# SwiGLU products and transposes later in their queues, activation sums between output-projection chunks, weight differences in place, in one layer on one Trainium2 core

## The chip, the core and the metric

The kernel runs on one core of a Trainium2 chip. The metric is the device time of one execution in microseconds (us); lower is better. Engines are named as in the profile: PE is TensorE's matmuls, PEld its weight loads, DVE is VectorE, ACT is ScalarE, POOL is GpSimd, and SP is SyncE, whose queue issues almost all loads.

## What is computed

The reference is one layer on 256 tokens of width 2048: a normalisation, an input projection into three token mixers (RWKV-7, gated delta rule, differential attention), an output projection with a residual, a second normalisation and a SwiGLU feed-forward part of hidden width 5632 with a residual. The change lies in the last third:

```
x = x + mixed @ w_out[l]
h = rms_norm(x, ffn_norm_w[l])
gate, up = jnp.split(h @ w_ffn_in[l], 2, axis=-1)
x = x + (jax.nn.silu(gate) * up) @ w_ffn_out[l]
```

All of it is in 32-bit floats.

## The kernel before, in words

**Products in three parts.** A 32-bit operand is split into a rounded part (hi, a cast on ACT) and a residual (lo, a subtraction on DVE), and a product is three matmuls: hi with hi, hi with lo, lo with hi. Each weight therefore goes through four steps: a load into a raw tile by SP's queue, the cast on ACT, the residual on DVE, and the matmuls of 128x128 by 128x512 on PE. The raw, hi and lo tiles rotate: 4 of each up to the feed-forward part, and there 5 raw (TILES["raw"] is 1), 8 hi and 8 lo.

**Before the feed-forward part.** The output projection has two halves of four chunks of 512 columns, oA and oB (the loop after `until("x2")`). After each chunk of oB, h2_cols (line 1220) is spawned: it turns the new columns of the residual stream by PE transposes and writes hTh and hTl, the split input of the feed-forward part. A spawned job is a Python generator; tick() moves every job one step, and a tick comes after each unit of weights, so a job's instructions stand between the units' instructions in the queues.

**The feed-forward part.** The hidden width is 11 chunks of 512. Chunk 0 is first_pair (line 1431): a gate projection and an up projection of 8 units each, 12 matmuls a unit. Chunks 1 to 10 are pair (line 1449, "pair 1" to "pair 10" below). A pair has 8 units of weights, each of two k-tiles of gate and up columns, and they alternate in kind. An S unit uses seven block products instead of eight, 21 matmuls; it needs sums of activation blocks and sums of weight blocks. An N unit has 24 matmuls and needs differences of activations. The seven partial results go to seven PSUM banks (four of mm, two of rw, one of gd) and are combined on DVE into the gate and up values of both token halves; ACT applies SiLU.

The groups in GROUPS say how the output products are interleaved: pair 1, four output units, pair 2, four output units, pair 3, eight output units, and so on with eight; after pair 10 come the last 24. An output unit (P) has two tiles of w_ffn_out and 12 matmuls.

**hid_cols** (line 1420) is spawned after each pair. Its first tick, after the next unit of PE work, multiplies gate by up (two DVE operations that write tile sg), the second and third tick turn the product by four PE transposes each into a gd bank, from which ACT and DVE write hidh and hidl, the split hidden values.

**Staging.** take_f (line 1339) is called ahead of each unit's matmuls and stages as many further units as the 8 hi and lo tiles allow; stage_one (line 1355) issues a unit's casts and residuals and load (line 1326) its successors' transfers. An N or P unit is a cast and a residual for each raw tile. An S unit (tiles b11, b12 | b21, b22) has four casts on ACT and seven operations on DVE: two that make b22 - b12 and that plus b11 in tile ta, two residuals, one that subtracts the sum from the second raw tile into tb, and the residuals of ta and tb.

**Activation sums.** ext_job (line 1395) is spawned before first_pair and makes the sums and differences of activations in 16 ticks, one pair of k-tiles in two ticks; finish(ej) runs what is left of it after first_pair.

**Order.** From `V.on = S.on = TE.on = True` on, that is in the whole feed-forward part, a helper (class Queue, line 98; its call is line 108, and nearly all instructions of the profile show that line) pins DVE, ACT and PE to the order in which the source issues instructions. The loop over seq sets that order:

```
            if ul is None:
                ej = spawn(ext_job())
                ab_ = first_pair(plan["first"])
                finish(ej)
            else:
                ab_ = pair(ul)
            spawn(hid_cols(ab_, hids[gi], j))
```

and in hid_cols the two multiplications come at the first step and a `yield` before each group of transposes. So in each queue a pair's multiplications stand after the first unit that follows the pair, and after what take_f staged ahead of that unit; the transposes stand after the second and the third.

Of the kernel before, what the change touches and what calls it, by code (L numbers as in the profile page):

```python
# [36 lines left out]
TILES = {"raw": 1, "hi": 4, "lo": 4}  # L37
# [116 lines left out]
def trunk(tc, A, out, dbg=None):  # L154
# [213 lines left out]
    lora = p_l.tile([P, 512], F32, name="lora")  # L368
    glora = p_l.tile([P, 512], F32, name="glora")
# [3 lines left out]
    gneps_c = C("eps")[:, 1:2]  # L373
    lnsc_c = C("eps")[:, 2:3]
# [93 lines left out]
    sgx = prq.tile([P, T], F32, name="sgx")  # L468
    bon = prq.tile([P, 4, T], F32, name="bon")
    Yt = prq.tile([P, 2, 512], F32, name="Yt")  # L470
    gns = prq.tile([P, 2, 24], F32, name="gns")
# [341 lines left out]
    cm_g2, pg2 = pool("gdn2", side="right")  # L813
    vtok = pg2.tile([P, 2, 4, 128], F32, name="vtok")
# [250 lines left out]
    def diff_evac(j, banks, res):  # L1065
        qns = []
        for t in range(2):
# [5 lines left out]
            ss = pd_.tile([P, 8], F32, tag="dss", name=nm("dss"), bufs=2)  # L1073
# [161 lines left out]

    until("x2")
# [3 lines left out]
    for key in ("oA", "oB"):  # L1240
        if key == "oB":
            finish(sj)
        for n in range(4):
# [16 lines left out]
    for cm in (cm_d, cm_mixrg, cm_rq, cm_tok, cm_l):  # L1260
        close(cm)
# [6 lines left out]
    NS = len(SEVEN)  # L1268
    sums_h = pf.tile([P, NS, 4, P], F32R, name="sums_h")
    sums_l = pf.tile([P, NS, 4, P], F32R, name="sums_l")  # L1270
    dif_h = pf.tile([P, KT // 2 - NS, 2, P], F32R, name="dif_h")
    dif_l = pf.tile([P, KT // 2 - NS, 2, P], F32R, name="dif_l")

# [35 lines left out]
    turn = {"raw": 0, "hi": 0, "lo": 0}  # L1309
    homes = {"raw": (p_raw, F32), "hi": (p_hi, F32R), "lo": (p_lo, F32R)}  # L1310

    def buf(kind):
        first, dt = homes[kind]
        i = turn[kind] % (4 + TILES[kind])
        turn[kind] += 1
        if i < 4:
            return first.tile([P, 1024], dt, tag=kind, name=nm(kind))
        return pf.tile([P, 1024], dt, tag=kind, name=nm(kind), bufs=TILES[kind])

    loaded, ready_w = {}, {}  # L1320
    at = {"load": 0, "stage": 0, "raw": 0, "cooked": 0, "used": 0}
# [4 lines left out]
    def load():  # L1326

        while at["load"] < len(queue) and at["raw"] + len(queue[at["load"]][1]) <= 4 + TILES["raw"]:
# [26 lines left out]
    def stage_one():  # L1355
# [3 lines left out]
        if kind != "S":  # L1359
            parts_ = [split(t) for t in r]  # L1360
            for x in parts_:
                x[2]()
            ready_w[u] = [half(x, j) for x in parts_ for j in range(2)]
        else:
# [15 lines left out]
            ready_w[u] = {"b11": half(s0, 0), "b21": half(s1, 0), "b22": half(s1, 1), "t3": half(sa, 0),  # L1380
                          "t2": half(sa, 1), "t4": half(sb, 0), "t1": half(sb, 1)}
# [3 lines left out]
        load()  # L1385

# [8 lines left out]
    def ext_job():  # L1395

        for q in range(KT // 2):
            x = pf.tile([P, 1024], F32, tag="ta", name=nm("xa"), bufs=1)[:, 0:2 * T].rearrange("p (k t) -> p k t", t=T)
            s_ = pf.tile([P, 512], F32, tag="u2", name=nm("xs"), bufs=1).rearrange("p (k t) -> p k t", t=P)
            V.tensor_tensor(x, hTh[:, 2 * q:2 * q + 2, :].bitcast(F32), hTl[:, 2 * q:2 * q + 2, :].bitcast(F32),  # L1400
                            op=ALU.add)
            if q in SEVEN:
                i = SEVEN.index(q)
                a11, a21, a12, a22 = x[:, 0, 0:P], x[:, 0, P:T], x[:, 1, 0:P], x[:, 1, P:T]
                V.tensor_tensor(s_[:, 0, :], a21, a22, op=ALU.add)
                V.tensor_tensor(s_[:, 2, :], a11, a21, op=ALU.subtract)
                V.tensor_tensor(s_[:, 1, :], s_[:, 0, :], a11, op=ALU.subtract)
                V.tensor_tensor(s_[:, 3, :], a12, s_[:, 1, :], op=ALU.subtract)
                h_, l_ = sums_h[:, i], sums_l[:, i]
            else:  # L1410
                i = [k for k in range(KT // 2) if k not in SEVEN].index(q)
                s_ = s_[:, 0:2, :]
                V.tensor_tensor(s_, x[:, :, 0:P], x[:, :, P:T], op=ALU.subtract)
                h_, l_ = dif_h[:, i], dif_l[:, i]
            yield
            S.copy(h_, s_)
            V.tensor_tensor(l_, s_, h_.bitcast(F32), op=ALU.subtract)
            yield
# [12 lines left out]
    def first_pair(ul):  # L1431
# [3 lines left out]
        for t in range(2):  # L1435
            sg = pf.tile([P, 512], F32, tag=f"sg{t}", name=nm("sg"), bufs=1)
# [3 lines left out]
        for i in range(len(uu)):  # L1440
            products(banks, uu, i, hx)
            if i == len(uu) - 4:
                load()
            if i == len(uu) - 2:
                stage_one()
            tick()
        return list(zip(sgs, banks))

    def pair(ul):
# [7 lines left out]
        for i, (u, q) in enumerate(ul):  # L1457
# [3 lines left out]
            if q in SEVEN:  # L1461
                e = SEVEN.index(q)
                s1, s2, s3, s4 = [(sums_h[:, e, j, :], sums_l[:, e, j, :]) for j in range(4)]
# [15 lines left out]
            if q == s_units[-1]:  # L1479
                c11 = pf.tile([P, 512], F32, tag="sg0", name=nm("sg"), bufs=1)  # L1480
                u2 = pf.tile([P, 512], F32, tag="u2", name=nm("u2"), bufs=1)
                u3 = pf.tile([P, 512], F32, tag="sg1", name=nm("sg"), bufs=1)
# [3 lines left out]
        c22 = pf.tile([P, 512], F32, tag="c22", name=nm("c22"), bufs=1)  # L1486
# [10 lines left out]
    for what, gi, j, ul in seq:  # L1497
        if what == "in":
            if j == 0:
                hids.append([pf.tile([P, 8, T], F32R, tag=tag, name=nm(tag), bufs=2) for tag in ("hidh", "hidl")])  # L1500
# [22 lines left out]
    for cm in (cm_f, R["x2"], cm_hT, cm_lo, cm_hi, cm_raw, cm_gdp, cm_rwp, cm_mm, cm_const):  # L1523
# [51 lines left out]
```

## Time and profile before

| | |
|---|---|
| median of 3 runs | 1238.4 us (1237.74 to 1238.54) |
| the profiled execution | 1237.4 us |
| its span, first to last instruction | 1235.5 us |
| PE busy | 1203.8 us, 97% |
| DVE busy | 946.6 us, 77% |
| ACT busy | 649.6 us, 53% |
| chain that ended last | PE 86%, DVE 8%, issue 3%, DMA 2%, ACT 2% |
| granted PE clock, mean | 0.995 |

The profile shows one execution. Busy time is the time in which an engine works on an instruction; matmuls are pipelined, and one that lasts 0.39 us can be followed by the next after less than that. An idle time of an engine carries the name of what ended it (the releaser). [...] The feed-forward part fills the span from about 493 us on; first_pair ends at about 537, pair 1 at 585, pair 2 at 643, pair 3 at 702.

### The profile page before, as it was taken

How to read it: one execution, taken by the hardware profiler on the slowest of the kernel's cores; microseconds unless marked ns; L12 is line 12 of the kernel's file. 1: busy time of each engine (PE TensorE's matmuls, PEld its weight loads, DVE VectorE, ACT ScalarE, POOL GpSimd, SP SyncE). 2: the span in 40 equal slices, each digit the busy share in tenths (PEclk: the TensorE clock that was granted, in tenths of full speed). 3: DMA queues.
4: the chain of work that ended last, by engine and by line, in shares of the span. 5: the costliest groups of instructions: out<-in, count | busy, mean ns of one | idle time of the engine just before them, and what ended most of it. 6: DMA issues, size and time to landing. Idle time of an engine off the chain costs nothing.

```text
span 1235.5 us, 16564 instructions
## 1 busy us (share of the span) xinstructions
PE 1203.8 (97%) x5942; PEld 985.9 (80%) x5942; DVE 946.6 (77%) x1310; ACT 649.6 (53%) x897; POOL 5.8 (0%) x11
## 2 busy tenths in 40 slices
PE   9999999999999999989898999999999999999998
PEld 7877888888888878868687788787878787878787
DVE  8585965699465767888989788887878796969852
ACT  7664454765456556645554445454645454545530
POOL 0100000000000000000000000000000000000000
PEclk9999999999999999999999999999999999999999
DMA  9755564256555536656465657475656565656761
GB/s 316 213 151 155 170 191 118 69 165 177 176 173 168 188 126 189 202 163 208 158 201 169 219 158 236 138 224 167 216 166 212 172 205 176 213 191 183 231 199 51
DMA packets 129201, 222.47 MB, mean 180 GB/s; under 512 B 19648, under 2 KB 24000, under 8 KB 129120
## 3 DMA queue, kind: packets, MB, share of 16 engines
q1 hardware_dynamic: 120960, 217.17, 56.4%
q10 hardware_dynamic: 8160, 4.27, 1.2%
q8 instruction: 46, 0.75, 0.2%
q14 instruction: 35, 0.29, 0.1%
HBM read 218.50 MB, written 2.88 MB: 179 GB/s over the span
## 4 chain that ended last, share of the span: by engine, by line
PE 86%; DVE 8%; issue 3%; DMA 2%; ACT 2%; DVEq 0%; SPq 0%; ACTq 0%
PE mm L108 71%; PE rw L108 9%; PE gd L108 6%; DVE lo L108 4%; DVE sg L108 2%; ACT hi L108 1%; DMA raw<-in_w_ffn_in 1%; DVE u L108 1%; DMA raw<-in_w_in 0%; DVE tb L108 0%; DMA vec<-in_vecs 0%; DVE c L108 0%; ACT s L108 0%; DVE ta L108 0%; DVEq L108 0%
## 5 line engine op out<-in xcount | busy, mean ns | idle before, releaser
L108 DVE TENSOR_TENSOR lo<-raw,hi 128x1024 fp32r<-128x1024 f32 (+2 forms) x410 | 461.6, 1152 | 134.0 <-ACT hi L108 133.5
L108 ACT CAST hi<-raw 128x1024 fp32r<-128x1024 f32 (+2 forms) x410 | 397.8, 994 | 259.3 <-PE mm L108 152.5
L108 PE MATMUL mm<-hi,hTh 128*128 128x512 f32 (+1 forms) x832 | 322.8, 394 | 1.0 <-ACT hi L108 1.0
L108 PE MATMUL mm<-lo,hTh 128*128 128x512 f32 (+1 forms) x832 | 317.1, 387 | 0.0
L108 PE MATMUL mm<-hi,hTl 128*128 128x512 f32 (+1 forms) x832 | 316.9, 387 | 0.0
L108 PEld LDWEIGHTS mm<-hi,hTh 128*128 128x128 f32 x832 | 155.4, 188 | 33.9 <-ACT hi L108 1.3
L108 PEld LDWEIGHTS mm<-hi,hTl 128*128 128x128 f32 x832 | 155.3, 188 | 32.4 <-issue 0.6
L108 PEld LDWEIGHTS mm<-lo,hTh 128*128 128x128 f32 x832 | 155.6, 188 | 30.9 <-issue 1.1
L108 PE MATMUL mm<-hi,hidh 128*128 128x512 f32 x352 | 140.8, 400 | 0.1
L108 PE MATMUL mm<-hi,hidl 128*128 128x512 f32 x352 | 138.6, 394 | 0.0
L108 PE MATMUL mm<-lo,hidh 128*128 128x512 f32 x352 | 138.6, 394 | 0.0
L108 PEld LDWEIGHTS mm<-hi,hidh 128*128 128x128 f32 x352 | 66.9, 190 | 16.5 <-issue 3.4
L108 PEld LDWEIGHTS mm<-hi,hidl 128*128 128x128 f32 x352 | 66.9, 190 | 14.5
L108 ACT CAST hi<-tb 128x1024 fp32r<-128x1024 f32 x40 | 42.2, 1054 | 68.8 <-DVE tb L108 67.2
L108 PEld LDWEIGHTS mm<-lo,hidh 128*128 128x128 f32 x352 | 66.8, 190 | 13.2
L108 ACT CAST hi<-ta 128x1024 fp32r<-128x1024 f32 x40 | 42.0, 1050 | 36.5 <-DVE ta L108 34.8
L108 DVE SCALAR_TENSOR_TENSOR xr<-mm,rst,xr 128x512 f32<-128x512 f32 x48 | 35.4, 748 | 27.5 <-PE mm L108 26.7
L108 DVE TENSOR_TENSOR lo<-tb,hi 128x1024 fp32r<-128x1024 f32 x40 | 49.0, 1225 | 3.7 <-ACT hi L108 1.3
L108 DVE TENSOR_TENSOR tb<-raw,ta 128x1024 f32<-128x1024 f32 x40 | 48.7, 1218 | 0.0
L108 DVE TENSOR_TENSOR lo<-ta,hi 128x1024 fp32r<-128x1024 f32 x40 | 48.7, 1217 | 0.0
L108 ACT CAST hidh<-gd 128x512 fp32r<-128x512 f32 x22 | 12.9, 587 | 62.1 <-PE gd L108 62.1
L108 DVE TENSOR_TENSOR hidl<-gd,hidh 128x512 fp32r<-128x512 f32 x22 | 15.2, 692 | 35.9 <-ACT hidh L108 35.8
(327 smaller groups left out, 1490.3 us busy)
## 6 DMA issues: line engine op xcount, KB each, us to landing
raw<-in_w_ffn_in SPq DMA_DIRECT2D x320, 256.0 KB, 3.2
raw<-in_w_in SPq DMA_DIRECT2D x103, 512.0 KB, 3.7
raw<-in_w_ffn_out SPq DMA_DIRECT2D x176, 256.0 KB, 3.9
raw<-in_w_out SPq DMA_DIRECT2D x32, 512.0 KB, 4.0
raw<-in_w_ffn_in SPq DMA_DIRECT2D x16, 512.0 KB, 3.9
raw<-in_w_in SPq DMA_DIRECT2D x9, 256.0 KB, 5.8
xr<-in_x SPq DMA_DIRECT2D x8, 256.0 KB, 5.4
out<-xr ACTq DMA_DIRECT2D x8, 256.0 KB, 2.1
```

The costliest lines, as they stand in the source:

```text
L108: r = call(*a, **kw)
```

## The change

- hid_cols gets an argument late. For pairs 1 to 10 it lets one tick pass ahead of the multiplications and one more ahead of the transposes: multiplications after the second following unit, transposes after the fourth and fifth. After first_pair the multiplications are issued at once (one step at spawn), the transposes stand where they stood.
- The activation sums move from ext_job into ext(n), which follows h2_cols(n) as one job (cols_ext) spawned after each chunk of oB, four k-tiles a part. The part of the last chunk runs in first_pair, which finishes it after the first unit of its up projection.
- In stage_steps (stage_one in steps) the weight differences of an S unit are written over the raw tiles; ta and tb are gone. The order of DVE is now difference, residual, sum, residual, subtraction, residual, residual. The first S unit is staged in steps during first_pair's up projection.
- Six raw tiles instead of five. To make room the pools of the earlier part stay open, and their tiles get new uses: sums and differences in old attention tiles, raw and lo tiles in the old constants and recurrence tiles, the hidden values alternately in an old and a new tile.
- The three epsilon columns get a DMA of their own into a small tile, behind that of the constants.

```diff
-TILES = {"raw": 1, "hi": 4, "lo": 4}
+TILES = {"raw": 2, "hi": 4, "lo": 4}
...
-    cst = p_l.tile([P, 1168], F32, name="cst")
-    eps_c = C("eps")[:, 0:1]
...
+    cst = p_l.tile([P, 1152], F32, name="cst")
+    eps_c, gneps_c, lnsc_c = drv[:, 48:49], drv[:, 49:50], drv[:, 50:51]
...
-        nc.sync.dma_start(cst[:, 0:CONST.shape[1] - P], A["const"][:, P:])
+        nc.sync.dma_start(cst, A["const"][:, P:P + 1152])
+        nc.sync.dma_start(drv[:, 48:51], A["const"][:, P + 1152:])
...
+    def ext(n):
+
+        x4 = prq.tile([P, 4, T], F32, tag="bon", name=nm("xa"))
+        s4 = prq.tile([P, 2, 4, P], F32, tag="Yt", name=nm("xs"))
+        V.tensor_tensor(x4, hTh[:, 4 * n:4 * n + 4, :].bitcast(F32), hTl[:, 4 * n:4 * n + 4, :].bitcast(F32),
+                        op=ALU.add)
+        yield
+        ss = []
+        for j, q in enumerate((2 * n, 2 * n + 1)):
+            x, s_ = x4[:, 2 * j:2 * j + 2, :], s4[:, j]
+            if q in SEVEN:
...
+            yield
+        for s_, h_, l_ in ss:
+            S.copy(h_, s_)
+            V.tensor_tensor(l_, s_, h_.bitcast(F32), op=ALU.subtract)
+            yield
+
+    def cols_ext(n):
+        yield from h2_cols(n)
+        yield
+        yield from ext(n)
...
             if key == "oB":
-                hj = spawn(h2_cols(n))
+                hj = spawn(cols_ext(n))
...
-            ta = pf.tile([P, 1024], F32, tag="ta", name=nm("ta"), bufs=1)
-            tb = pf.tile([P, 2, 512], F32, tag="tb", name=nm("tb"), bufs=1)
-            V.tensor_tensor(ta[:, 0:512], b22, b12, op=ALU.subtract)
-            V.tensor_tensor(ta[:, 512:1024], ta[:, 0:512], b11, op=ALU.add)
+            V.tensor_tensor(b12, b22, b12, op=ALU.subtract)
             s0[2]()
+            yield
+            V.tensor_tensor(b11, b12, b11, op=ALU.add)
             s1[2]()
-            sa = split(ta)
-            V.tensor_tensor(tb, r[1].rearrange("p (a c) -> p a c", c=512),
-                            ta[:, 512:1024].unsqueeze(1).to_broadcast([P, 2, 512]), op=ALU.subtract)
-            sb = split(tb.rearrange("p a c -> p (a c)"))
+            yield
+            sa = split(r[0])
+            two = r[1].rearrange("p (a c) -> p a c", c=512)
+            V.tensor_tensor(two, two, b11.unsqueeze(1).to_broadcast([P, 2, 512]), op=ALU.subtract)
+            yield
+            sb = split(r[1])
             sa[2]()
+            yield
             sb[2]()
...
-    def hid_cols(ab_, hid, c):
+    def hid_cols(ab_, hid, c, late):
+        if late:
+            yield
         for x, y in ab_:
             V.tensor_tensor(x, x, y, op=ALU.mult)
+        yield
         for i in range(2):
             yield
             b = gdbank(1)
...
             products(banks, uu, i, hx)
+            if i == 0:
+                finish(hj)
+                early = spawn(stage_steps())
             if i == len(uu) - 4:
+                at["limit"] = len(queue)
                 load()
             if i == len(uu) - 2:
+                finish(early)
                 stage_one()
             tick()
...
             if ul is None:
-                ej = spawn(ext_job())
                 ab_ = first_pair(plan["first"])
-                finish(ej)
             else:
                 ab_ = pair(ul)
-            spawn(hid_cols(ab_, hids[gi], j))
+            spawn(hid_cols(ab_, hids[gi], j, late=ul is not None), 0 if ul is not None else 1)
```

## Rows read from the trace of the kernel before

**Rows 1.** Page, part 1: busy us (share of the span) xinstructions.
```profile
PE 1203.8 (97%) x5942; PEld 985.9 (80%) x5942; DVE 946.6 (77%) x1310; ACT 649.6 (53%) x897; POOL 5.8 (0%) x11
```
**Rows 2.** Waits of PE: us in total, times, longest.
```profile
PE gd L108 <- DVE sg L108: 20.4, 20, 4.3
```
**Rows 3.** Timeline of PE, 540 to 710: start, us, what, [idle before, releaser].
```profile
545.19 0.76 PE L108 MATMUL mm<-hi,sums_h 128*128 128x512 f32 x1 [4.58 <-DVE sg L108]
...
595.23 0.30 PE L108 MATMUL gd<-ident,sg 128*128 128x128 f32 x1 [4.32 <-DVE sg L108]
...
653.14 0.30 PE L108 MATMUL gd<-ident,sg 128*128 128x128 f32 x1 [3.06 <-DVE sg L108]
...
709.63 0.30 PE L108 MATMUL gd<-ident,sg 128*128 128x128 f32 x1 [1.37 <-DVE sg L108]
```
**Rows 4.** Windows: length, busy PE, PEld, DVE, ACT, POOL, then clock, DMA share, GB/s.
```profile
545.00:550.00 5.00, 4.81 (x14) 3.86 (x15) 4.96 (x8) 1.09 (x2) 0.00 (x0) 0.66 0.82 262
595.00:600.00 5.00, 4.56 (x14) 3.58 (x15) 3.74 (x6) 2.48 (x3) 0.00 (x0) 0.66 0.00 1
653.00:658.00 5.00, 4.64 (x15) 3.63 (x16) 3.74 (x6) 2.48 (x3) 0.00 (x0) 0.66 0.00 0
709.00:714.00 5.00, 4.16 (x22) 3.41 (x23) 1.77 (x3) 0.67 (x2) 0.00 (x0) 1.00 0.60 201
464.00:496.00 32.00, 32.00 (x154) 26.38 (x153) 24.01 (x33) 21.76 (x40) 0.00 (x0) 1.00 0.63 185
...
1225.00:1230.00 5.00, 5.00 (x24) 4.14 (x23) 0.00 (x0) 0.00 (x0) 0.00 (x0) 1.00 0.00 0
```
**Rows 5.** Timeline of PE and DVE around the first two stalls.
```profile
539.53 0.69 DVE L108 TENSOR_TENSOR xa<-hTh,hTl 128x512 f32<-128x512 f32 x1
...
544.36 1.28 DVE L108 TENSOR_TENSOR sg<-sg,mm 128x512 f32<-128x512 f32 x2
...
585.21 0.47 PE L108 MATMUL mm<-hi,hidh 128*128 128x512 f32 x1
...
587.37 0.68 DVE L108 TENSOR_TENSOR ta<-raw,raw 128x512 f32<-128x512 f32 x1
...
595.00 0.68 DVE L108 TENSOR_TENSOR sg<-sg,c 128x512 f32<-128x512 f32 x1
```
**Rows 6.** The chain that ended last, in order of time: its last long piece.
```profile
1174.34 57.17 PE mm L108 x252
```
**Rows 7.** Tile xs: its DVE operations, ns min/median/max, first and last start, forms.
```profile
L108 DVE TENSOR_TENSOR xs<-xa x12: 282/292/426, 496.4 to 540.2; 128x128 f32<-128x128 f32 x8, 128x256 f32<-128x256 f32 x4
...
L108 DVE TENSOR_TENSOR sums_l<-xs,sums_h x4: 683/690/693, 500.7 to 531.1; 128x512 fp32r<-128x512 f32 x4
...
L108 DVE TENSOR_TENSOR dif_l<-xs,dif_h x4: 417/418/424, 506.4 to 541.1; 128x256 fp32r<-128x256 f32 x4
```
**Rows 8.** Tile raw: its loads.
```profile
DMA to landing us min/median/max: 2.6/3.8/8.3
```
**Rows 9.** Timeline of PE and DVE in pair 2, and around a transpose group.
```profile
603.68 0.39 PE L108 MATMUL rw<-hi,hTh 128*128 128x512 f32 x1
...
604.55 0.68 DVE L108 TENSOR_TENSOR ta<-raw,raw 128x512 f32<-128x512 f32 x1
...
610.03 1.22 DVE L108 TENSOR_TENSOR lo<-tb,hi 128x1024 fp32r<-128x1024 f32 x1
...
613.88 0.39 PE L108 MATMUL rw<-hi,hTh 128*128 128x512 f32 x1
...
658.38 0.60 PE L108 MATMUL gd<-ident,sg 128*128 128x128 f32 x4
...
659.64 0.69 DVE L108 TENSOR_TENSOR hidl<-gd,hidh 128x512 fp32r<-128x512 f32 x1 [0.50 <-ACT hidh L108]
```
**Rows 10.** DMA issues: KB each, median us to landing.
```profile
raw<-in_w_in SPq DMA_DIRECT2D x2, 4.0 KB, 3.2
```
**Rows 11.** Timeline of ACT: its first use of the constants.
```profile
37.20 0.26 ACT L108 ACTIVATE rst<-rw,cst 128x2 f32<-128x2 f32 x1 [4.14 <-PE rw L108]
```

More of the change, by code (lines that the diff above doesn't have):

```diff
@@ L467, in trunk @@
     cm_rq, prq = pool("rwq")
-    sgx = prq.tile([P, T], F32, name="sgx")
+    sgx = p_l.tile([P, T], F32, tag="xs1", name="sgx")
     bon = prq.tile([P, 4, T], F32, name="bon")
     Yt = prq.tile([P, 2, 512], F32, name="Yt")
-    gns = prq.tile([P, 2, 24], F32, name="gns")
     cm_rw, pr = pool("rwp")
@@ L813, in trunk @@
     cm_g2, pg2 = pool("gdn2", side="right")
+    gns = pg2.tile([P, 2, 16], F32, name="gns")
     vtok = pg2.tile([P, 2, 4, 128], F32, name="vtok")
@@ L1072, in diff_evac @@
             qn = p_tok.tile([P, 512], F32, tag="tok", name=nm("qn"), bufs=TOKB)
-            ss = pd_.tile([P, 8], F32, tag="dss", name=nm("dss"), bufs=2)
+            ss = (ssq, drv[:, 52:60])[t]
             act(qn, b, AF.Square)
@@ L1234, in h2_cols, with old, small @@
                                        op0=ALU.mult, op1=ALU.subtract)
+    def ext(n):
[8 more added lines that the diff above has]
+            if q in SEVEN:
+                a11, a21, a12, a22 = x[:, 0, 0:P], x[:, 0, P:T], x[:, 1, 0:P], x[:, 1, P:T]
+                V.tensor_tensor(s_[:, 0, :], a21, a22, op=ALU.add)
+                V.tensor_tensor(s_[:, 2, :], a11, a21, op=ALU.subtract)
+                V.tensor_tensor(s_[:, 1, :], s_[:, 0, :], a11, op=ALU.subtract)
+                V.tensor_tensor(s_[:, 3, :], a12, s_[:, 1, :], op=ALU.subtract)
+                ss.append((s_, *sums[SEVEN.index(q)]))
+            else:
+                i = [k for k in range(KT // 2) if k not in SEVEN].index(q)
+                s_ = s_[:, 0:2, :]
+                V.tensor_tensor(s_, x[:, :, 0:P], x[:, :, P:T], op=ALU.subtract)
+                ss.append((s_, dif_h[:, i], dif_l[:, i]))
+            yield
[7 more added lines that the diff above has]
+        yield from ext(n)
+    def old(tag, shape):
+        return pd_.tile(shape, F32R, tag=tag, name=nm("sums"), bufs=2)
+    def small():
+        return p_tok.tile([P, 512], F32, tag="tok", name=nm("sm"), bufs=TOKB)
     until("x2")
@@ L1242, in trunk @@
             finish(sj)
+            sums_h, sums_l = [[old(tag, [P, 2, 4, P]) for _ in range(2)] for tag in ("dqk0", "dqk1")]
+            dif_h, dif_l = [old("dv", [P, KT // 2 - len(SEVEN), 2, P]) for _ in range(2)]
+            sums = [(sums_h[i // 2][:, i % 2], sums_l[i // 2][:, i % 2]) for i in range(len(SEVEN))]
         for n in range(4):
@@ L1259, in trunk @@
     close(R["dr"])
-    for cm in (cm_d, cm_mixrg, cm_rq, cm_tok, cm_l):
-        close(cm)
     cm_f, pf = pool("ffn")
@@ L1307, in trunk @@
         seq.append(("out", gi, n, plan_out(n, 4 * (c0 - ng), 4 * ng)))
-    turn = {"raw": 0, "hi": 0, "lo": 0}
-    homes = {"raw": (p_raw, F32), "hi": (p_hi, F32R), "lo": (p_lo, F32R)}
+    first = {"raw": [(p_l, "loras", 1), (p_l, "cst", 1)], "hi": [], "lo": [(prq, "bon", 1), (prq, "Yt", 1)]}
+    homes = {}
+    for kind, old_ in (("raw", p_raw), ("hi", p_hi), ("lo", p_lo)):
+        more = TILES[kind] - len(first[kind])
+        homes[kind] = first[kind] + [(pf, kind, more)] * more + [(old_, kind, 4)] * 4
+    turn = {kind: 0 for kind in homes}
     def buf(kind):
-        first, dt = homes[kind]
-        i = turn[kind] % (4 + TILES[kind])
+        home, tag, n = homes[kind][turn[kind] % len(homes[kind])]
         turn[kind] += 1
-        if i < 4:
-            return first.tile([P, 1024], dt, tag=kind, name=nm(kind))
-        return pf.tile([P, 1024], dt, tag=kind, name=nm(kind), bufs=TILES[kind])
+        return home.tile([P, 1024], F32 if kind == "raw" else F32R, tag=tag, name=nm(kind), bufs=n)
     loaded, ready_w = {}, {}
-    at = {"load": 0, "stage": 0, "raw": 0, "cooked": 0, "used": 0}
+    at = {"load": 0, "stage": 0, "raw": 0, "cooked": 0, "used": 0, "limit": 1}
     def need(u):
@@ L1326, in load @@
     def load():
-        while at["load"] < len(queue) and at["raw"] + len(queue[at["load"]][1]) <= 4 + TILES["raw"]:
+        while at["load"] < min(len(queue), at["limit"]) and at["raw"] + len(queue[at["load"]][1]) <= 4 + TILES["raw"]:
             tiles = []
@@ L1385, in stage_one @@
         load()
+    def stage_one():
+        for _ in stage_steps():
+            pass
     def triple(bank, a, w, start, stop):
@@ L1435, in first_pair @@
         for t in range(2):
-            sg = pf.tile([P, 512], F32, tag=f"sg{t}", name=nm("sg"), bufs=1)
+            sg = small()
             act(sg, bg[t], AF.Silu, scale=rs2[:, t:t + 1])
@@ L1462, in pair @@
                 e = SEVEN.index(q)
-                s1, s2, s3, s4 = [(sums_h[:, e, j, :], sums_l[:, e, j, :]) for j in range(4)]
+                s1, s2, s3, s4 = [(sums[e][0][:, j, :], sums[e][1][:, j, :]) for j in range(4)]
                 f7, l7 = q == s_units[0], q == s_units[-1]
@@ L1479, in pair @@
             if q == s_units[-1]:
-                c11 = pf.tile([P, 512], F32, tag="sg0", name=nm("sg"), bufs=1)
-                u2 = pf.tile([P, 512], F32, tag="u2", name=nm("u2"), bufs=1)
-                u3 = pf.tile([P, 512], F32, tag="sg1", name=nm("sg"), bufs=1)
+                c11 = small()
+                u2 = small()
+                u3 = small()
                 S.copy(c11, p1)
@@ L1485, in pair @@
                 V.tensor_tensor(u3, u2, p7, op=ALU.add)
-        c22 = pf.tile([P, 512], F32, tag="c22", name=nm("c22"), bufs=1)
+        c22 = small()
         V.tensor_tensor(c11, c11, p2, op=ALU.add)
@@ L1499, in trunk @@
             if j == 0:
-                hids.append([pf.tile([P, 8, T], F32R, tag=tag, name=nm(tag), bufs=2) for tag in ("hidh", "hidl")])
+                hids.append([(p_mixrg, pf)[gi % 2].tile([P, 8, T], F32R, tag=tag, name=nm(tag), bufs=1)
+                             for tag in ("mixh_a", "mixl_a")])
             if ul is None:
-                ej = spawn(ext_job())
                 ab_ = first_pair(plan["first"])
-                finish(ej)
             else:
                 ab_ = pair(ul)
-            spawn(hid_cols(ab_, hids[gi], j))
+            spawn(hid_cols(ab_, hids[gi], j, late=ul is not None), 0 if ul is not None else 1)
         else:
@@ L1522, in trunk @@
                     nc.scalar.dma_start(out_v[t][:, 512 * j:512 * (j + 1)], o)
-    for cm in (cm_f, R["x2"], cm_hT, cm_lo, cm_hi, cm_raw, cm_gdp, cm_rwp, cm_mm, cm_const):
+    for cm in (cm_f, R["x2"], cm_d, cm_mixrg, cm_rq, cm_tok, cm_l, cm_hT, cm_lo, cm_hi, cm_raw, cm_gdp, cm_rwp, cm_mm, cm_const):
         close(cm)
```

39 lines of the change are left out of this document (5 added, 34 removed).

## The prediction

> **What bounds the kernel now.** I read the engine line of the page first: TensorE (PE) is busy 1203.8 us of the 1235.5 us span, 97% [rows 1]. So at most 32 us can come from removing waits, whatever VectorE (DVE) or the DMA queues save, unless matmuls themselves run faster. The second view is the list of PE's waits: 20 waits of gd on DVE sg add up to 20.4 us [rows 2]. The gd matmuls behind sg are the transposes of hid_cols, and sg is what its SwiGLU multiplications write. The third view, PE's timeline, says where: one stall of 4.58 us behind the first pair, in which mm waits for sg, then for gd one behind pair 1 (4.32), one behind pair 2 (3.06), and one of about 1.37 behind each of pairs 3 to 10, of which one stands here; each transpose group has a second wait of about 0.21 for the second multiplication, counted in the 20.4 [rows 3]. The fourth view is the granted clock. [...]
>
> Why sg is late is seen in DVE's queue, whose order the source fixes in this stage. Pair 1's output units start on PE at 585.21, and the transposes stand behind the second of them. DVE first ends pair 1's additions, then runs all seven operations of the next S unit from 587.37, and only then the two multiplications, which end at 595.68 [rows 5]. A unit of 12 matmuls is 12 x 226.9 ns = 2.72 us by the last stretch of the chain, 252 matmuls in 57.17 us [rows 6]; two units are over at 590.7, and PE waits.
>
> [...] I take PE as the bound.
>
> **The change, part by part.** Transposes later. With late set, a pair's multiplications are issued after the second following unit instead of the first, and its transposes after the fourth and fifth instead of the second and third. That adds 2 x 2.72 = 5.4 us of PE work ahead of the transposes and moves the multiplications behind at most one more staged unit. Pairs 3 to 10 have no S unit between, so their 1.37 us vanish with 4 us to spare. For pairs 1 and 2 four units end at 585.21 + 10.9 = 596.1; the multiplications ended at 595.7 [rows 5] and may end some 0.4 later, since in place the second subtraction stands behind a residual that waits for ScalarE's cast. Between nothing and 0.7 us each is left; I take 0.3, together 0.6. Removed: 20.4.
>
> First pair. The multiplications are now issued at its end, ahead of pair 1's first unit. Before, the last of the activation sums, started again at 539.53, and two residuals stood ahead of them until 544.36 [rows 5], while the sixth product group waited for the bank that they read. That bank is wanted after 15 matmuls (3.4 us); two multiplications take 1.28 us [rows 5]. Removed: 4.6.
>
> Clock. Without the three stalls longer than 3 us, nothing there lowers it: 3 x 5 us x (1 - 0.66) = 5.1 us [rows 4]. The 1.37 us stalls give none back.
>
> Activation sums earlier. A part for four k-tiles is one 128x1024 addition of some 1.22 us, as such operations take [rows 9], four 128x128 operations of 0.29, one 128x256 of 0.42, and residuals of 0.69 and 0.42 [rows 7], 3.9 us on DVE. Of the four parts, two and the addition of a third fall between output-projection chunks: 2 x 3.9 + 1.2 = 9.0 us. DVE was busy 24.0 of 32 us there [rows 4], so it is asked for 33.0: one us too much. Weights are staged three units ahead, 8.2 us, of which cast and residual take some 2.3, so a backlog of up to 5.9 us is covered. Cost taken: 0. Uncovered it would be from 1.0 to 9.0 us, plus 1.7 for the clock; a gain is excluded, since PE never waits there now. The rest falls in the first pair, where DVE loses 9.0 us of work; staging the first S unit early needs only tiles that are long free.
>
> Weight differences in place. The same seven DVE and four ACT operations; nothing is saved. The two raw tiles of an S unit are held to its end instead of partly freed after the first residuals, and the sixth raw tile answers that: three two-tile units instead of two are in hand, and SyncE's queue asks for a unit while two others, over 9 us of DVE work, are still to be staged, against a landing of 3.8 us [rows 8]. Cost taken 0; bounds 0 and 3.8 us for each of 40 S units.
>
> Pairs 2 and 3's second S unit. After the two short output groups the second transpose now stands behind the first unit of the next pair, and DVE and ACT can't stage the next S unit before it. That staging began at 604.55, 0.9 us after PE's unit at 603.68; now it begins after that unit (4.8 us), four transposes, a cast and a residual: a transpose group at 658.38 has its residual started at 659.64 and done 0.7 later [rows 9]. So it is some 6 us later. Its last residual ended at 611.25, and PE wants that group 3.4 us after 613.88 [rows 9], also 0.4 later now. 617.7 - 617.3 = 0.4 us to spare. Cost taken 0; bounds 0 and 2 us for each of two pairs.
>
> Epsilon columns. They get a small DMA of their own on SyncE's queue behind the constants. No row shows one of 12 bytes a partition; the nearest is one of 4 KB in all, 3.2 us to landing [rows 10]. ACT's first use waited 4.14 us for PE, not for the constants [rows 11], which covers that; behind it stand the identity and the low-rank weights, which are used later. Cost taken 0; bounds 0 and 3.2 us. GpSimd's queue is passed by nothing. The other moves of tiles issue nothing.
>
> **Sum.** 20.4 + 4.6 + 5.1 - 0.6 = 29.5 us. The profiled execution took 1237.4 us (1.9 beside its span), 1.0 under the median of 1238.4. Against the profile that is 1207.9, against the median **1208.9 us**.
>
> **Rivals.** *VectorE too full between output-projection chunks*: the 1.0 us overrun grows past the staging lead and PE waits there. For it: 33.0 of 32. Against: DVE's idle time before may also have been spent on work that can slide. 1208.9 + 2.7 to 10.7, some 1215.
>
> *A new wait at pairs 2 and 3* for the late S unit: 0.4 us to spare is less than my reckoning is good for. Up to 2 x 2 us, and 1.7 of clock for each stall if it becomes long: 1210 to 1216.
>
> *Slower: raw tiles come back too late.* An S unit (604.55 to 611.25) and an N unit's two residuals take DVE 6.7 + 2 x 1.22 = 9.1 us, and PE 10.2 (603.68 to 613.88 [rows 9]). If the longer hold lays a landing of 3.8 us [rows 8] open in each couple, it takes 12.9; 40 couples by 2.7 cost 108 us, and the time is 1317. It decides from 29.5 / 40 = 0.74 us a couple. Against it: the sixth tile, and a lead of over 9 us.
>
> *Nothing moves*: the hardware order stays, or another resource paces PE. The time is 1238. Against: the order in this stage is the source's, and [rows 4, 6].
>
> **How the numbers follow.** Forecast 0.70, full VectorE 0.13, pairs 2 and 3 0.08, slower 0.05, nothing 0.04. A difference under 0.2%, some 2.5 us, can't be told from none. The first three cases are faster: 0.91; same 0.04; slower 0.05. Low end: all waits gone without the 0.6, and 1.8 us for what the runs scatter and for the 2 us that PE still idles at the start: 1206.5. High end: 1217, which takes in the second rival and most of the first; the two last, 0.09, and the first's tail stay out.
>
> **What would show it.** Right: no gd on sg in PE's waits, the clock at 1.00 from 540 to 660, the multiplications straight behind the first pair, the sums' rows from about 475 to 515, and a distance of 64.2 instead of 65.8 us between the stalls' former places. Full VectorE: waits of PE on hi or lo before 500. Raw tiles: ACT or DVE waiting for DMA raw. The prediction is wrong if PE's idle time in sum stays over 12 us, or if matmuls start more than 227 ns apart without a wait.

## The result and the profile after

The changed kernel takes 1211.66 us (median of 4 runs, 1208.73 to 1212.23) against 1238.45 us: a ratio of 0.978 [0.9763, 0.9797] (the brackets hold a 95% interval, here and below), 26.8 us less. The forecast was 1208.9, with 1206.5 to 1217.0. The direction and the range hold; the point is 2.8 us too low. The profiled execution took 1212.02 us.

Two lines of the page of after: the engine line, which answers to [rows 1], and the chain.

```profile
PE 1198.6 (99%) x5942; PEld 985.1 (81%) x5942; DVE 942.7 (78%) x1306; ACT 650.2 (54%) x897; POOL 5.8 (0%) x11
...
PE 87%; DVE 6%; DMA 3%; issue 2%; ACT 2%; SPq 0%; DVEq 0%; ACTq 0%
```

PE is still the bound, now at 99%. The waits of PE in after (us in total, times, longest) answer to [rows 2]:

```profile
PE mm L108 <- DVE sm L108: 3.3, 2, 3.0
PE mm L108 <- ACT hi L108: 1.5, 1, 1.5
PE rw L108 <- DVE xs L108: 1.2, 1, 1.2
PE mm L108 <- DVE xr L108: 1.0, 1, 1.0
PE rw L108 <- DVE s L108: 0.3, 1, 0.3
```

All 20 waits of gd on the multiplications are gone. (Tiles share old homes now: sm stands for sg, mixh_a and mixl_a for hidh and hidl, sums for sums_h, sums_l, dif_h and dif_l.) Two waits are new and not small, and PE's timeline has them at two hand-offs, the start of pair 2 and the end of pair 3; it answers to [rows 3] (its first row, the transposes behind pair 1, has no wait):

```profile
590.97 0.60 PE L108 MATMUL gd<-ident,sm 128*128 128x128 f32 x4
...
595.96 0.47 PE L108 MATMUL mm<-hi,sums 128*128 128x512 f32 x1 [0.96 <-DVE xr L108]
...
690.12 0.77 PE L108 MATMUL mm<-hi,mixh_a 128*128 128x512 f32 x1 [2.98 <-DVE sm L108]
690.68 0.63 PE L108 MATMUL mm<-lo,mixh_a 128*128 128x512 f32 x1
691.11 0.63 PE L108 MATMUL mm<-hi,mixl_a 128*128 128x512 f32 x1
```

Behind the second of them matmuls start 0.43 us apart, against 0.227 [rows 6]. Windows of after, with the columns of [rows 4]:

```profile
464.00:496.00 32.00, 32.00 (x154) 26.38 (x153) 29.60 (x49) 23.05 (x42) 0.00 (x0) 1.00 0.64 193
...
690.00:692.00 2.00, 1.88 (x5) 1.52 (x6) 2.00 (x4) 0.72 (x1) 0.00 (x0) 0.50 1.05 390
692.00:694.00 2.00, 2.00 (x6) 1.61 (x5) 0.37 (x1) 1.60 (x3) 0.00 (x0) 0.50 0.71 261
694.00:696.00 2.00, 2.00 (x6) 1.52 (x6) 1.91 (x2) 1.00 (x2) 0.00 (x0) 0.50 0.04 16
696.00:698.00 2.00, 2.00 (x10) 1.62 (x9) 1.66 (x3) 0.00 (x0) 0.00 (x0) 0.96 0.76 243
```

The three low-clock stretches of [rows 4], with a mean of 0.66, are gone (1.00 from 540 to 550, 595 to 600 and 653 to 658), but after the new 2.98 us stall PE runs some 6 us at a granted clock of 0.50, half of full speed (690.12 to about 696.1). That costs about 2.9 us: the eight output units behind pair 3 take 25.69 us, where those behind pairs 4 to 9 take 22.84. The first window is the stretch of oB: DVE is busy 29.6 of 32 us there (24.0 before), and PE waits for nothing.

**Where the time went.** The table takes each block from its first matmul in PE's timeline to the first matmul of the next. O1 is the output units behind pair 1, and so on; "forecast" puts the terms of the prediction where they belong.

| block | before, us | after, us | gain | forecast |
|---|---|---|---|---|
| up to first_pair | 492.57 | 493.27 | -0.70 | 0 |
| first_pair and pair 1 | 92.64 | 86.71 | 5.93 | 6.3 |
| O1 and pair 2 | 18.47 + 40.80 | 11.35 + 42.61 | 5.31 | 5.93 |
| O2 and pair 3 | 17.09 + 40.97 | 11.24 + 44.94 | 1.88 | 4.67 |
| O3 | 24.81 | 25.69 | -0.88 | 1.58 |
| pair 4 to the last output chunks, 7 waits | 504.15 | 490.33 | 13.82 | 11.06 |
| sum | | | 25.4 | 29.5 |

The sum is that of the two profiled executions; before's lies 1.05 us under its median and after's 0.36 over, which makes the 26.8. Two rows carry the miss (O2 with pair 3, and O3: 5.3 us), and one gives 2.8 back.

**What a wait is worth.** O4 to O9 shrink from 24.81 to 22.84, 1.97 us for each pair of waits, which I had put at 1.37 + 0.21 = 1.58. PE's timeline of before, around the stall whose row stands in [rows 3], shows why:

```profile
707.87 0.39 PE L108 MATMUL mm<-hi,hidl 128*128 128x512 f32 x1
...
710.14 0.55 PE L108 MATMUL gd<-ident,sg 128*128 128x128 f32 x3 [0.21 <-DVE sg L108]
710.44 0.48 PE L108 MATMUL mm<-hi,hidh 128*128 128x512 f32 x1
...
713.28 0.60 PE L108 MATMUL gd<-ident,sg 128*128 128x128 f32 x4
713.64 0.48 PE L108 MATMUL mm<-hi,hidh 128*128 128x512 f32 x1
```

The unhindered group of transposes takes 713.64 - 713.28 = 0.36 us, and a matmul ahead of it 0.23, so the way from the last matmul to the next output matmul is 0.59 us. Behind the wait it took 710.44 - 707.87 = 2.57: 1.98 us lost, 0.40 more than the idle time. An idle time counts from the modelled end of a matmul (0.39 us behind its start), 0.16 after the point where the next would have started in the rows ahead (0.23 behind it). The other 0.24 went at the restart of the transposes: from the first of them at 709.63 to the output matmul at 710.44 are 0.81 us, less the second wait of 0.21 that is 0.60, against the unhindered 0.36.

### The profile page after: what moved, and what is told of

Same layout as the page of the kernel before. It is cut to its first block, busy times and chain, and to the rows that moved or that the text cites. A ratio compares the mean times of both kernels' runs of the same rounds, so it can differ in the third digit from the quotient of the medians.

```text
span 1210.0 us, 16543 instructions
## 1 busy us (share of the span) xinstructions
PE 1198.6 (99%) x5942; PEld 985.1 (81%) x5942; DVE 942.7 (78%) x1306; ACT 650.2 (54%) x897; POOL 5.8 (0%) x11
## 4 chain that ended last, share of the span: by engine, by line
PE 87%; DVE 6%; DMA 3%; issue 2%; ACT 2%; SPq 0%; DVEq 0%; ACTq 0%
PE mm L108 74%; PE rw L108 9%; PE gd L108 5%; DVE lo L108 3%; DMA raw<-in_w_ffn_out 1%; DVE raw L108 1%; ACT hi L108 1%; DMA raw<-in_w_ffn_in 1%; DMA raw<-in_w_in 1%; DVE xr L108 0%; DVE sm L108 0%; DMA vec<-in_vecs 0%; ACT s L108 0%; ACT mixh_a L108 0%; DVE mixl_a L108 0%
## 5 line engine op out<-in xcount | busy, mean ns | idle before, releaser
L108 ACT CAST hi<-raw 128x1024 fp32r<-128x1024 f32 (+1 forms) x490 | 478.5, 1004 | 336.3 <-DVE raw L108 127.9
L108 DVE TENSOR_TENSOR lo<-raw,hi 128x1024 fp32r<-128x1024 f32 (+1 forms) x490 | 558.8, 1164 | 115.1 <-ACT hi L108 109.6
L108 PE MATMUL mm<-hi,mixh_a 128*128 128x512 f32 x416 | 166.4, 400 | 3.3 <-DVE sm L108 3.3
L108 PE MATMUL mm<-hi,mixl_a 128*128 128x512 f32 x416 | 163.3, 393 | 0.0
L108 PE MATMUL mm<-lo,mixh_a 128*128 128x512 f32 x416 | 163.1, 392 | 0.0
L108 PE MATMUL mm<-hi,sums 128*128 128x512 f32 x320 | 118.2, 390 | 1.1 <-DVE xr L108 1.0
L108 PEld LDWEIGHTS mm<-hi,mixh_a 128*128 128x128 f32 x416 | 78.8, 189 | 23.4 <-issue 7.9
L108 PEld LDWEIGHTS mm<-hi,mixl_a 128*128 128x128 f32 x416 | 78.8, 189 | 17.0
L108 PEld LDWEIGHTS mm<-lo,mixh_a 128*128 128x128 f32 x416 | 78.9, 190 | 15.6
L108 DVE TENSOR_TENSOR raw<-raw,raw 128x512 f32<-128x512 f32 x80 | 76.3, 954 | 1.3
```

What stands on the lines that cost most here:

```text
L108: r = call(*a, **kw)
```

## The experiments

Every time is a median, beside a median of the kernel before on the same chip (1238.6, 1239.7 or 1239.2 us). The hand-off theory of the expectations: the late transposes themselves make the hand-offs to pairs 2 and 3 late, since their residuals stand ahead of staging in DVE's queue. Its rivals are the raw-hold theory (the longer hold of the raw tiles) and chance.

**after_again**: the changed kernel, unchanged.

> The changed kernel once more. Two theories of what kept it 2.8 us above the forecast, where the profile shows PE waiting 0.96 us for xr in pair 2 and 2.98 us for sm at the end of pair 3, with 3 us at the low clock behind the latter. Hand-off theory: the residual of the second transposes stands behind the first unit of pairs 2 and 3, VectorE stages all of the pair late, raw tiles come back late and the output weights land late; every execution has both waits, 1211 to 1212. Raw-hold theory: holding raw tiles to the end of an S unit makes the loads of output weights late in itself; every execution has the wait at the end of pair 3, 1211 to 1212. Rival of both, chance: the landing of a few transfers varies, and an execution without the long wait and its low clock takes 1206 to 1209.

1209.7 us (1208.61 to 1212.2), 0.9766 [0.975, 0.9781]. The two new waits recur. PE's timeline of this run:

```profile
594.68 0.47 PE L108 MATMUL mm<-hi,sums 128*128 128x512 f32 x1 [0.96 <-DVE xr L108]
...
689.90 0.77 PE L108 MATMUL mm<-hi,mixh_a 128*128 128x512 f32 x1 [4.04 <-DVE sm L108]
```

and its windows behind the second:

```profile
690.00:692.00 2.00, 2.00 (x5) 1.62 (x6) 2.00 (x4) 0.51 (x1) 0.00 (x0) 0.50 0.96 327
692.00:694.00 2.00, 2.00 (x8) 1.56 (x8) 0.27 (x2) 1.83 (x3) 0.00 (x0) 0.76 0.30 111
694.00:696.00 2.00, 2.00 (x11) 1.65 (x10) 2.00 (x2) 0.79 (x1) 0.00 (x0) 1.00 0.01 2
```

The waits belong to the kernel, not to one execution: every profile below that keeps the late transposes behind pair 2 and the staging ahead has a stall at the end of pair 3. The low clock behind the longer stall is shorter here, about 3 us. The eight executions of both labels sort by the clock: three at a mean clock of 1.000 took 1208.6 to 1209.0 us, three at 0.996 or 0.997 took 1212.0 to 1212.2, two at 0.999 lie between. A high clock doesn't mean that the long wait is absent: raw_five below has it (2.71 us) in an execution at 1.000.

**late_alone**: before, with the late steps of hid_cols alone; sums, weight differences and raw tiles as they were.

```diff
-            spawn(hid_cols(ab_, hids[gi], j))
+            spawn(hid_cols(ab_, hids[gi], j, late=ul is not None))
...
+        if late:
+            yield
         for x, y in ab_:
             V.tensor_tensor(x, x, y, op=ALU.mult)
+        if late:
+            yield
```

> The kernel before with one part of the change: for pairs 1 to 10 the multiplications one unit and the transposes two units later. Prediction's terms: the waits of gd on sg go (20.4 us) and two of the three stretches at the low clock (3.4), while the 4.6 us stall behind the first pair and its 1.7 us stay: 1238.5 - 23.8 = 1214.7. Theory that each wait also cost a restart of 0.4 us (the eight short ones took 1.97 us of block length for 1.58 of wait): 4 us more, 1210.7. Hand-off theory: this part alone brings the late staging of pairs 2 and 3 with it, with waits of PE on xr or sg there, 3 to 8 us back, 1214 to 1219. Raw-hold theory: the late staging needs the in-place edit, so no such waits here, 1210 to 1212.

1215.13 us (1214.38 to 1216.34), 0.981 [0.9796, 0.9823]. Waits of PE in this run:

```profile
PE mm L108 <- DVE sg L108: 7.6, 2, 4.6
...
PE mm L108 <- DVE xr L108: 0.9, 2, 0.5
```

The 7.6 are 4.58 behind first_pair, as in [rows 3], and 3.04 at the end of pair 3 (695.12). The hand-off waits come with the late transposes alone, without in-place differences: the raw hold is not their cause. The time decides less than the waits do, since the prediction's terms (1214.7) and the hand-off theory (1214 to 1219) both allow it. Late steps alone gain 24.5 us.

**late_undone**: after, with the multiplications and transposes of pairs 1 to 10 where they stood.

```diff
-            spawn(hid_cols(ab_, hids[gi], j, late=ul is not None), 0 if ul is not None else 1)
+            spawn(hid_cols(ab_, hids[gi], j, late=False), 0 if ul is not None else 1)
...
-        yield
+        if c == 0 and hid is hids[0]:
+            yield
         for i in range(2):
```

> The changed kernel with that part undone: multiplications after the first, transposes after the second and third unit behind pairs 1 to 10. If the late transposes carry the gain, the 20 waits of gd on sm return with about 20 us, two low-clock stretches and the restarts, less the 8 us of the waits in pairs 2 and 3 that the late transposes made: 1230 to 1235. Rival: the early sums and the sixth raw tile do most of it, and the time is under 1225.

1233.39 us (1232.66 to 1234.29), 0.9957 [0.9943, 0.997]. Its waits of PE begin with

```profile
PE gd L108 <- DVE sm L108: 21.4, 19, 4.8
```

The old waits are back, and the hand-off waits are gone. By blocks of the profiled execution, first_pair and pair 1 take 86.49 us against 92.64 before, so 6.15 us of the gain stay there; the prediction put stall and clock at 4.6 + 1.7 = 6.3. (The medians differ by 6.3 us too, but not for this alone: O1 and O2 are 1.6 us longer than before's, and the executions of before on that chip scatter from 1237.3 to 1240.3.)

**sums_undone**: after, with the activation sums in first_pair again and the first S units staged whole at its end (cols_ext becomes h2_cols, a job over all four parts is spawned in first_pair).

```diff
-                hj = spawn(cols_ext(n))
+                hj = spawn(h2_cols(n))
...
+        ej = spawn(ext_all())
...
-                finish(hj)
-                early = spawn(stage_steps())
...
-                finish(early)
+                finish(ej)
+                stage_one()
                 stage_one()
```

> The changed kernel with the activation sums made in the first pair again and the first S unit staged at its end. If the early sums are what frees VectorE at the end of the first pair, PE waits there for weights of the S unit or for the bank, 3 to 6 us plus 1.7 of clock: 1214 to 1219. If it is only the place of the multiplications that matters, 1209 to 1211.

1215.23 us (1212.71 to 1216.29), 0.9807 [0.9792, 0.9822]. In PE's timeline the stall in pair 1 is back, if shorter:

```profile
544.06 0.47 PE L108 MATMUL mm<-hi,sums 128*128 128x512 f32 x1 [2.74 <-DVE sm L108]
```

first_pair and pair 1 take 91.75 us against 86.50 in after_again. So this part of the change is worth about 5.2 us in that block. The edit undoes two things at once (sums, and staging in steps); which of them the multiplications need was not tried apart.

**raw_five**: after, with at most five raw tiles in hand.

```diff
-... at["raw"] + len(queue[at["load"]][1]) <= 4 + TILES["raw"]:
+... at["raw"] + len(queue[at["load"]][1]) <= 5:
```

> The changed kernel with at most five raw tiles in hand instead of six. This prices the prediction's slower rival, in which raw tiles held to the end of an S unit come back too late. Raw-hold theory: after an S unit only the N unit behind it (2.4 us on VectorE) is left while the next S unit's data need 3.8 us or more to land, so each couple of units takes 9.1 + 2 = 11 us against 10.2 on PE; 40 couples by 0.8 are 32 us less what the output blocks give back: 1220 to 1242, with ACT waiting for DMA raw in all pairs. If the sixth tile is not needed: 1208 to 1213, as the changed kernel.

1209.62 us (1207.71 to 1211.43), 0.9765 [0.975, 0.978]: as after_again, with the same two waits of PE (0.96, and 2.71 at 688.64). One line of its waits, ACT's for the output weights (20.9 us, 21 times in after):

```profile
ACT hi L108 <- DMA raw<-in_w_ffn_out: 16.8, 24, 1.7
```

The sixth raw tile buys nothing that can be measured, and in-place differences do not need it.

**at_once_12**: after, with pairs 1 and 2 multiplied at once and turned after the second and third unit.

```diff
-            spawn(hid_cols(ab_, hids[gi], j, late=ul is not None), 0 if ul is not None else 1)
+            spawn(hid_cols(ab_, hids[gi], j, late=gi > 1), 0 if gi > 1 else 1)
```

> After pairs 1 and 2 the multiplications are issued at once, ahead of the next S unit, and the transposes stand after the second and third output unit, so no residual waits behind the next pair's first unit. Hand-off theory: the waits of PE for xr (0.96 us) and sm (2.98 us) and the low clock vanish, and PE has no wait over 0.5 us from 540 on; 1212.0 less 0.96, 2.98, 3.1 and two restarts of 0.4 is 1204.2, so 1203.5 to 1206. Raw-hold theory: the wait for sm at the end of pair 3 stays between 2 and 4 us, and only the 1.4 of the xr wait goes; 1210 to 1211.5. A cost of the edit itself: VectorE idles about 1 us for SiLU before the multiplications, and the S unit comes some 2 us later than in the changed kernel.

1208.28 us (1207.96 to 1210.68), 0.9756 [0.9741, 0.977]. Both hand-off waits are gone, that at the end of pair 3 too, though pair 3's own product is treated as in after: what differs at pair 3's start are pair 2's transposes, which in after stand behind its first unit. (The edit frees both hand-offs at once, so pair 1's share isn't separated.) The time is still 2.3 us above the expected 1203.5 to 1206, since PE's timeline has a new wait in their place:

```profile
591.81 0.66 PE L108 MATMUL gd<-ident,sm 128*128 128x128 f32 x4 [2.23 <-DVE mixl_a L108]
```

and DVE's timeline of the same run says why:

```profile
588.65 2.50 DVE L108 TENSOR_TENSOR lo<-raw,hi 128x1024 fp32r<-128x1024 f32 x2
591.07 0.68 DVE L108 TENSOR_TENSOR mixl_a<-gd,mixh_a 128x512 fp32r<-128x512 f32 x1
```

The second transposes need the gd bank of the first, whose residual stands behind an S unit. In the profiled execution, the slowest (1210.68 us), matmuls also start 0.43 us apart for about 3 us behind this wait (592.63 to 595.61; 0.227 in [rows 6]); the other three kept a mean clock of 1.000.

**adds_first**: after, with nothing staged ahead in a pair's last unit, so that the pair's additions on DVE come ahead of the residuals of the next unit.

```diff
-    def take_f(u):
+    def take_f(u, ahead=True):
-        while at["stage"] < len(queue) and (at["stage"] <= u or
+        while at["stage"] < len(queue) and (at["stage"] <= u or ahead and
...
-            w = take_f(u)
+            w = take_f(u, ahead=i < len(ul) - 1)
```

> The last unit of a pair stages nothing ahead, so the additions that end a pair stand ahead of the residuals of the later output weights instead of behind up to four of them. The transposes stay as in the changed kernel. Hand-off theory: the loads of output weights are still late after pair 3, but the additions no longer wait for them, so PE's wait for sm goes; the wait for xr in pair 2 stays. 1212.0 less 2.98, 3.1 and 0.4 is 1205.5; 1205 to 1207.5. Raw-hold theory: the weights are late by the same 3 us and PE waits for lo or hi of an output unit instead; 1209 to 1212.

1209.68 us (1208.74 to 1210.89), 0.9766 [0.9752, 0.9779]. Its waits of PE:

```profile
PE gd L108 <- DVE sm L108: 3.9, 6, 1.4
PE mm L108 <- DVE xr L108: 1.9, 2, 1.0
```

The stall at the end of pair 3 is gone, so DVE's order there was its immediate cause. The time, however, is that of after_again, above the expected 1205 to 1207.5: staging left for later pushes the multiplications of pairs 1, 2 and 10 back behind it (1.44 us twice and 0.36 once, each with a second wait), and the wait for xr now stands at pair 3 as well as at pair 2.

**both_fixes**: the edits of at_once_12 and adds_first together.

> Both edits. Hand-off theory: nothing is left for the second edit after the first, 1203.5 to 1206, the same as the first alone within 0.1%. Raw-hold theory: 1208 to 1211, and PE waits for lo or hi of output units. If both matter separately, this one is over 1 us faster than either alone.

1215.24 us (1213.29 to 1217.5), 0.9808 [0.9792, 0.9824], and a miss: no theory had a time above 1211, and the edits do not add, they harm each other. Its waits of PE begin with

```profile
PE gd L108 <- DVE mixl_a L108: 7.2, 2, 3.6
```

It is the wait for the gd bank of at_once_12, grown from 2.23 and 0.98 to 3.59 and 3.57 us: the two residuals of output weights that adds_first leaves for later now stand ahead of the S unit, and so of the residual that frees the bank, while PE comes there no later.

**two_banks**: at_once_12, with the two transpose groups of pairs 1 and 2 in different gd banks.

```diff
-    def hid_cols(ab_, hid, c, late):
+    def hid_cols(ab_, hid, c, late, other=False):
...
-            b = gdbank(1)
+            b = gdbank(1 - i if other else 1)
...
-            spawn(hid_cols(ab_, hids[gi], j, late=ul is not None), 0 if ul is not None else 1)
+            spawn(hid_cols(ab_, hids[gi], j, late=gi > 1, other=gi == 1), 0 if gi > 1 else 1)
```

> As the kernel with multiplications at once after pairs 1 and 2 (median 1208.3), in which PE waited 2.23 and 0.98 us because the second transposes there need the gd bank whose residual stands behind the next S unit; here they use the other gd bank. Hand-off theory: no wait of PE over 0.5 us is left from 540 on; the output blocks behind pairs 1 and 2 shrink from 15.96 and 13.04 us to 11.7 each: 1202.6, so 1201.5 to 1204.5. Raw-hold theory: waits for weights come up in pairs 2 and 3, 1205 to 1208.

1206.08 us (1205.41 to 1208.02), 0.9737 [0.9724, 0.9751]: faster than after, but above the expected 1201.5 to 1204.5 and in the range of the raw-hold theory (1205 to 1208), whose waits for weights are not there. PE's timeline has one wait left in the feed-forward part, at the fourth of pair 2's seven products:

```profile
595.02 0.50 PE L108 MATMUL gd<-hi,sums 128*128 128x512 f32 x1 [1.21 <-DVE mixl_a L108]
```

That product needs the bank of the second transposes, so what was taken from the transposes is partly asked back there. Another part of the miss lies in the expectation's sum: it took the 15.96 us of O1 from the execution of 1210.68 us with its low clock, and subtracted from the median, 1208.3, of executions of which most had none.

**two_banks_adds**: two_banks, and the edit of adds_first for pairs 3 to 9 alone, where it made no new waits.

```diff
-            w = take_f(u)
+            w = take_f(u, ahead=i < len(ul) - 1 or ended in (1, 2, 10))
...
-                ab_ = pair(ul)
+                ab_ = pair(ul, 2 * gi - 1 + j)
```

> The kernel with two banks (1206.1), and in pairs 3 to 9 the last unit of a pair stages nothing ahead, so that the pair's additions don't stand behind residuals of output weights. In the kernel with that edit alone each output block behind pairs 4 to 9 was 0.12 us shorter and each pair 0.17 us: 7 x 0.29 = 2.0 us, 1204.1; 1203.5 to 1205.5. If the additions had been in time anyway: 1206.

1204.08 us (1203.21 to 1204.2), 0.9721 [0.9708, 0.9734]: the fastest of all, as expected. All that PE still waits for, beside xs (1.2) and s (0.3) ahead of the feed-forward part as in every run:

```profile
PE gd L108 <- DVE mixl_a L108: 1.1, 1, 1.1
PE mm L108 <- ACT hi L108: 0.5, 1, 0.5
```

Its range is 1.0 us wide where that of after is 3.5: with the long stall the low-clock stretch is gone too (mean clocks of 0.999 and 1.000).

## Why the prediction was right, and where it failed

**The bound.** Right. PE's waits fall to 7.3 us in sum, under the 12 that I named, and the time follows them. The rival in which another resource paces PE (1238) falls with the time; in [rows 4, 6] PE also takes 226.9 ns a matmul, in a stretch that holds 5 us without work on DVE, ACT or the DMA engines.

**The 20 waits, 20.4 us.** Right in kind: none is left, and late_undone brings them back. The size was too low, by 0.4 us a pair of waits, since I took idle time for lost time; the row of seven waits gained 13.82 us instead of 11.06. The 0.6 us set aside for late multiplications behind pairs 1 and 2 was not needed: the transposes at 590.97 follow the unit ahead of them without a wait.

**First pair, 4.6 us, and its clock, 1.7.** Right, by late_undone (6.15 us in that block) and sums_undone (5.2). DVE's timeline of after has the first and last rows of the sums and the multiplications straight behind first_pair, where [rows 5] had them at 544.36:

```profile
473.28 1.22 DVE L108 TENSOR_TENSOR xa<-hTh,hTl 128x1024 f32<-128x1024 f32 x1
...
515.74 0.42 DVE L108 TENSOR_TENSOR sums<-xs,sums 128x256 fp32r<-128x256 f32 x1
...
536.59 0.69 DVE L108 TENSOR_TENSOR sm<-sm,mm 128x512 f32<-128x512 f32 x1 [1.72 <-PE mm L108]
537.95 0.69 DVE L108 TENSOR_TENSOR sm<-sm,mm 128x512 f32<-128x512 f32 x1 [0.67 <-PE mm L108]
538.55 0.69 DVE L108 TENSOR_TENSOR raw<-raw,raw 128x512 f32<-128x512 f32 x1
```

**Sums between chunks, cost 0.** Right. The rows of the sums ahead of 496 us do add up to the 9.0 us that I had added, but DVE's busy time rose by only 5.6, to 29.6 of 32: rows of DVE overlap, by 1.9 us more than before, 0.3 us of the sums stood there before, and 1.1 us of other work left the window. The rival of a full VectorE falls: PE never waits there.

**In place, cost 0.** Right, for a weaker reason than mine: I let the sixth tile answer for the longer hold, and raw_five shows that five do. The slower rival (1317 us) falls with it: raw_five took 1209.62. The epsilon columns show in no wait.

**Clock, 5.1 us.** The three stretches went as forecast, but "nothing there lowers it" was wrong: behind the new stall of 2.98 us at the end of pair 3 PE ran some 6 us at a granted clock of 0.50 in the profiled execution, 2.9 us lost.

**Pairs 2 and 3's second S unit, "0.4 us to spare. Cost taken 0".** This is the step that failed. I had followed the late residual to one reader, the second S unit. What stands behind it in DVE's queue is more, as DVE's timeline of after at the start of pair 2 (591.33) shows:

```profile
592.20 2.35 DVE L108 TENSOR_TENSOR lo<-raw,hi 128x1024 fp32r<-128x1024 f32 x2
594.47 0.69 DVE L108 TENSOR_TENSOR mixl_a<-gd,mixh_a 128x512 fp32r<-128x512 f32 x1
595.07 1.40 DVE L108 SCALAR_TENSOR_TENSOR xr<-mm,rst,xr 128x512 f32<-128x512 f32 x2
598.68 0.69 DVE L108 TENSOR_TENSOR mixl_a<-gd,mixh_a 128x512 fp32r<-128x512 f32 x1 [2.21 <-ACT mixh_a L108]
599.29 0.68 DVE L108 TENSOR_TENSOR raw<-raw,raw 128x512 f32<-128x512 f32 x1
```

The additions of O1 to the residual stream (595.07), which free an mm bank, stand behind two residuals of a staged unit and that of the first transposes; PE needs the bank at once and waits 0.96 us. Then DVE stands 2.21 us for ACT, which casts the second transposes (on PE from 597.43), and the S unit starts at 599.29, 8.0 us into the pair instead of 0.9 [rows 9]; I had said some 6 later, and it is 7.1.

At pair 3 (from 645.18) the S unit starts 7.2 us into the pair in the same way, where it was 0.9 before. It follows DVE's wait of 2.22 us for the cast of pair 2's second transposes, and no wait of PE is listed there:

```profile
652.34 0.68 DVE L108 TENSOR_TENSOR raw<-raw,raw 128x512 f32<-128x512 f32 x1
```

The price comes due where I didn't look, at that pair's end. ACT's timeline there:

```profile
682.87 1.06 ACT L108 CAST hi<-raw 128x1024 fp32r<-128x1024 f32 x1 [1.72 <-DMA raw<-in_w_ffn_out]
685.73 1.05 ACT L108 CAST hi<-raw 128x1024 fp32r<-128x1024 f32 x1 [1.80 <-DMA raw<-in_w_ffn_out]
687.08 1.04 ACT L108 CAST hi<-raw 128x1024 fp32r<-128x1024 f32 x1 [0.30 <-DMA raw<-in_w_ffn_out]
```

and DVE's:

```profile
686.81 2.57 DVE L108 TENSOR_TENSOR lo<-raw,hi 128x1024 fp32r<-128x1024 f32 x2 [1.49 <-ACT hi L108]
689.30 3.07 DVE L108 TENSOR_TENSOR sm<-sm,mm 128x512 f32<-128x512 f32 x5
```

Staging is late, the output weights land late, their residuals stand in DVE's queue ahead of pair 3's additions, and PE's next output unit needs an mm bank that these free: 2.98 us. at_once_12 shows the first link and adds_first the last (S unit 8.0 us into pair 3, but additions ahead, no wait). In at_once_12 pair 3 starts at 650.50, its S unit 2.1 us later, and there is no wait at its end. The link between is in SyncE's timelines, of after and then of at_once_12:

```profile
669.33 13.79 SPq L1370 DMA_DIRECT2D raw<-in_w_ffn_out  x16
...
669.61 15.33 SPq L1370 DMA_DIRECT2D raw<-in_w_ffn_out  x16
```

The first output weights are asked for 24.2 us into pair 3 in after and 19.1 in at_once_12, 5 us apart like the S units. That this alone makes them land late is still an inference: in the windows around the stall the DMA engines are also at a share of 1.05 (688 to 692 in after), and neither was varied by itself.

So the rival of a new wait at pairs 2 and 3 (1210 to 1216) named the late S unit and the time, but not where it is paid: no wait stands at the second S unit itself, and PE waits for banks, not for weights. In the table the blocks from O1 to O3 fall short by 5.9 us, first_pair and the start by 1.1, and the underrated waits give 2.8 back: some 4.2 in the profiled executions. The executions that kept the clock at 1.000 took 1208.6 to 1209.0 us, on the forecast, but by two errors that cancel.

The subtraction at 599.29 needs nothing of the transposes, and it stands still for the 2.21 us that the residual ahead of it waits. (The source pins that order; what DVE would do without it was not shown.)

## What to carry to other kernels

A step that is moved later takes everything behind it with it in a queue whose order the source pins, as here: list what it will stand ahead of at each hand-off, and who waits for that, above all banks to be freed, and follow the lag to the next hand-off, not to its first reader alone. A removed wait was worth more here than the idle time in its row, by 0.4 us for a pair of short ones. Two reorderings that each take a wait away can harm together, so each is put only where its own wait was, as in two_banks_adds.

## What was unexpected of the hardware

A longer stall did not cost more clock: after 2.98 us of idle time PE ran about 6 us at a granted clock of 0.50, after 4.04 us in another execution of the same kernel about 3. Nor did the length of a stall decide whether matmuls slow down: after 2.23 us in at_once_12 they start 0.43 us apart (592.63 and 593.05), after 2.71 us in raw_five 0.23 (688.95 and 689.18), in an execution with a mean clock of 1.000. In the 6 us of after, too, matmuls start 0.43 us apart, where the last long stretch of before has 0.227 [rows 6].

PE's wait for the first weights (mm on ACT hi in the lists of waits) differs between executions with the same start of the program: 1.5 us in after, 0.3 in after_again, 2.8 in at_once_12. first_pair starts later with it, at 493.27, 492.21 and 494.19 us: a part of the scatter that no edit here touches.
